# Sixteen more gathers in the front, three of them in flight across a change of pools, and top-16 operations of several lists taking turns

## The chip, the cores and the metric

The kernel runs on one core of one Trainium2 chip. The metric is the device time of one execution in microseconds; the median of three runs is given. The engines are named as in the profile: PE (matrix multiplication), DVE (vector), ACT (activation functions), POOL (here it only issues gathers) and SP (it issues the other transfers).

## The reference

One decoder layer over 512 tokens of width 1024: an attention of two groups of eight heads, a projection, a layer norm, then a lookup of experts (PEER), and a layer norm.

```python
def hybrid_mixer(x, w_in, w_out):
    proj = x @ w_in                       # q, k, v of both head groups
    oa = dilated_window_attention(qa, ka, va)     # heads "a": three dilated windows
    ob = stick_breaking_attention(qb, kb, vb)     # heads "b": cumulative log-sigmoids
    return concat(merge_heads(oa), merge_heads(ob)) @ w_out

def peer_ffn(x, w_query, sub_keys, expert_u, expert_v):
    q = (x @ w_query).reshape(b, s_len, 8, 2, 128)
    scores = einsum('bshpc,hpnc->bshpn', q, sub_keys)      # two lists of 128 per head
    top_s, top_i = top_k(scores, 16)
    cand_s = top_s[..., 0, :, None] + top_s[..., 1, None, :]   # 256 candidates per head
    best_s, best_pos = top_k(cand_s.reshape(..., 256), 16)
    expert_idx = take_along_axis(cand_i, best_pos)          # 128 experts per token
    gates = softmax(best_s)
    h = einsum('td,ted->te', x, expert_u[expert_idx])
    return einsum('te,ted->td', gates * gelu(h), expert_v[expert_idx])

x = layer_norm(ALPHA * x + hybrid_mixer(x, ...))
x = layer_norm(ALPHA * x + peer_ffn(x, ...))
```

## The kernel before, in words

The 512 tokens are four blocks of 128 (tb 0 to 3). For blocks 0 and 1 the experts' rows are gathered: one gather brings, for each of 128 tokens, the row of its j-th expert, 128 x 1024 numbers, 512 KB. That is 128 gathers of `peer_u` and 128 of `peer_v` for each block, 512 in all (`NG`). `gathers` keeps up to GB1 - 1 = 4 of them in flight with the first set of buffers, and some more once a second set (`g2`) is open; POOL issues them (L706). `gather_use` consumes them on DVE: a multiply with a running sum for a u row (L715), a multiply-add for a v row (L724, the first one L721). After the last u row of a block a Gelu on ACT turns the sums into gates (L717). Blocks 2 and 3 go through all experts instead ("dense"): chunks of 128 experts, with h matmuls (L821) and y matmuls (L1074), and gates from one-hot matrices (the gate stage). "h parts" of this dense work are put into earlier stages by `run_ahead`.

In time the program goes so:

- Block 0 goes first alone: projection, heads, output projection, layer norm, query, top-16, routing (`route_steps`), so that its gathers can begin at about 150 us.
- The front, 200 to 298 us: block 0's first `PRE0` gathers, the input projection of blocks 1 to 3 (weights split in two parts, L124) and the dilated heads of blocks 1 and 2 take turns in the proportion `MIXB`. Up to here a scheduler that inserts waits works on the written order. `limit` says up to which gather issues are allowed. At the end the old pools are closed and those of the next stages opened in their memory.
- The attention loop, 298 to about 500 us, under a manual schedule: 32 tasks, a head each, first the dilated heads of block 3 ("a") and the stick-breaking heads of block 1 ("b") alternating, then those of blocks 2 and 3. Each task takes one, two or three gathers. DVE's operations for a head are the masks with maximum (L318), the log parts (L349), and a division (L365); PE's are L315, L325, L331 (dilated) and L339 to L359 (stick-breaking). `load_out` loads the output weights before the loop. From task 20 the output projection (L492) and the normalization of block 1 are filled in, from task 28 those of block 2.
- The query loop, 500 to 634 us: 18 steps; step `it` multiplies the query of one list for blocks 1 to 3 (`q_mm`), the scores of the list before (`q_scores`, L593), and the top-16 of the list before that (`topk16`, L524 to L528, once for each of three blocks), with a gather after each of the three and `QH` h parts at its end.
- `route_steps(2)`, 634 to 672 us; then the gate stage, 672 to 806 us, with `route_steps` of blocks 3 and 1 in it; the main loop over the chunks of experts with the remaining gathers, 826 to 1483 us; the end.

Each engine runs its instructions in its own order, which is the order of the code in the manually scheduled part. In the names of tiles `su` is a head's scores, `nm` the negative maximum, `g` a gathered row set, `hg` the running sums of the u rows, `x` block 0's tokens, `yg` a second accumulator, `sc` the scores of a list.

Of the kernel before, what the change touches and what calls it, by code (L numbers as in the profile page):

```python
# [10 lines left out]
F32 = mybir.dt.float32  # L11
# [5 lines left out]
OP = mybir.AluOpType  # L17
# [3 lines left out]
P = 128  # L21
S = 512
D = 1024
# [3 lines left out]
NH = 8  # L27
# [39 lines left out]
PARTS = (0,), (1, 2, 3)  # L67
# [9 lines left out]
PRE0 = 52  # L77
QGATH = 3
QH = 3
# [4 lines left out]
GB1, GB2 = 5, 4  # L84
NG = 4 * P
GEND = P - 8
WBUF = 4
# [6 lines left out]
def build(ctx, nc, tc, a):  # L94
# [61 lines left out]
    def stats_steps(st):  # L156
        mv = keep.tile([P, 2], F32, name="mv", bufs=2)
        nc.vector.bn_aggr(mv, st.rearrange("p a b -> p (a b)"))
        w = keep.tile([P, 4], F32, name="lw", bufs=2)
        nc.vector.tensor_scalar_add(w[:, 0:1], mv[:, 1:2], EPS)  # L160
        nc.scalar.activation(w[:, 1:2], w[:, 0:1], AF.Ln)
        nc.scalar.activation(w[:, 2:3], w[:, 1:2], AF.Exp, scale=-0.5)
        yield
# [316 lines left out]
    def load_out():  # L480
        for c in range(2):
            for kq in range(4):
                wo[c, kq] = wop.tile([P, 2, 512], F32, name=f"wo{c}{kq}")
                nc.sync.dma_start(wo[c, kq], a["w_out"][c, kq])

# [10 lines left out]
    def normalize(tb):  # L496
        t = [] if tb == 0 else ln1
        if not t:
            for n in ("ln1_g", "ln1_b"):
                t.append(wst.tile([P, D], F32, name="w", bufs=WBUF) if tb == 0 else wop.tile([P, D], F32, name=n))  # L500
                nc.sync.dma_start(t[-1], a[n].to_broadcast([P, D]))
        r = x2[:, tb]
        s_ = stats_steps(sts[tb])
        next(s_)
# [3 lines left out]
        for g in range(2):  # L508
            sl = slice(g * 512, (g + 1) * 512)
            nc.vector.scalar_tensor_tensor(r[:, sl], r[:, sl], mv[:, 0:1], t[0][:, sl], op0=OP.subtract, op1=OP.mult)  # L510
            nc.vector.scalar_tensor_tensor(r[:, sl], r[:, sl], rs, t[1][:, sl], op0=OP.mult, op1=OP.add)
# [10 lines left out]
    def topk16(tb, i, sc):  # L522
        s2 = rq.tile([P, P], F32, name="s2", bufs=3)
        nc.vector.max(top[tb][:, i, 0:8], sc)  # L524
        nc.vector.max_index(topi[tb][:, i, 0:8], top[tb][:, i, 0:8], sc)  # L525
        nc.vector.match_replace(s2, top[tb][:, i, 0:8], sc, FMIN)
        nc.vector.max(top[tb][:, i, 8:16], s2)
        nc.vector.max_index(topi[tb][:, i, 8:16], top[tb][:, i, 8:16], s2)  # L528

# [67 lines left out]
    def route_steps(tb, h0=0, n=PH):  # L597
# [4 lines left out]
        def rt(shape, nm, dt=F32):  # L602
            return rq.tile(shape, dt, name=nm, bufs=1)
# [14 lines left out]
        for h in range(n):  # L618
            c2 = rq.tile([P, NCAND], F32, name="c2", bufs=2)
            nc.vector.max(best[:, h, 0:8], cand[:, h])  # L620
            nc.vector.max_index(posu[:, h, 0:8], best[:, h, 0:8], cand[:, h])
            nc.vector.match_replace(c2, best[:, h, 0:8], cand[:, h], FMIN)
            nc.vector.max(best[:, h, 8:16], c2)
            nc.vector.max_index(posu[:, h, 8:16], best[:, h, 8:16], c2)
            yield
        gt_ = (gate0, gate1)[tb][:, ks].rearrange("p (h k) -> p h k", h=n) if tb < 2 else rt([P, n, 16], "gate")
        nc.vector.tensor_sub(gt_, best, best[:, :, 0:1].to_broadcast([P, n, 16]))
        pos = rt([P, NK], "pos")
        nc.vector.tensor_copy(pos, posu.rearrange("p h k -> p (h k)"))
        posb = rt([P, NK], "posb", BF16)  # L630
        nc.vector.tensor_copy(posb, pos)
        t64 = rt([P, n, 16], "t64")
        nc.vector.tensor_scalar_mul(t64, topf[:, :, 0], 64.0)
        d0 = rt([P, n, 16], "d0")
        nc.vector.tensor_copy(d0[:, :, 0:1], t64[:, :, 0:1])
        nc.vector.tensor_sub(d0[:, :, 1:16], t64[:, :, 1:16], t64[:, :, 0:15])
# [22 lines left out]
        nc.vector.reduce_sum(gz, gt_, axis=AX.X)  # L659
        nc.vector.reciprocal(gz, gz)  # L660
        nc.vector.tensor_mul(gt_, gt_, gz[:, :, None].to_broadcast([P, n, 16]))
        nc.vector.tensor_sub(bo, bo, pos)
        nc.vector.tensor_scalar(i1, bo, 1.0 / 64.0, MAGIC, op0=OP.mult, op1=OP.add)
# [65 lines left out]
    limit = 0  # L729
# [135 lines left out]
    limit = PRE0  # L865
# [31 lines left out]
    with tc.manual_schedule():  # L897
        def take(n):
            for _ in head(gs, n):
# [3 lines left out]
                 [(k_, 3 if k_ == "a" else 1, h) for h in range(NH) for k_ in "ab"] + [("b", tb, h) for tb in (2, 3) for h in range(NH)]]  # L903
# [3 lines left out]
        load_out()  # L907
        for i in range(-1, NTASK + 2):
# [3 lines left out]

            new = i + 1 < NTASK
# [25 lines left out]
            if (fill_at := {20: 1, 28: 2}.get(i)):  # L939
                fill = chain(fill, project_out(fill_at), normalize(fill_at))  # L940
# [24 lines left out]
        for it in range(18):  # L965
# [7 lines left out]
            if it >= 2:  # L973
                for t, tb in enumerate(PARTS[1]):
                    topk16(tb, it - 2, scs[it - 2][:, t])
                    if t < QGATH:
                        take(1)
            else:
                take(2)
# [226 lines left out]
```

## Time and profile before

| what | value |
|---|---|
| median of 3 runs | 1584.94 us (1584.32 to 1587.28) |
| profiled execution, own time | 1586.14 us |
| its span | 1584.3 us |
| granted PE clock, mean | 0.935 |
| PE busy | 1433.4 us (90%) |
| DVE busy | 1223.2 us (77%) |
| ACT busy | 507.8 us (32%) |
| POOL busy | 686.0 us (43%) |
| HBM read | 477.78 MB, 312 GB/s over the span |

The profile is one execution. A busy share is an average over stages with different limits; a stage is read by its own window. The granted clock is the share of full speed that the throttle let PE have. A line of waits says which engine and line waited for which engine and line: total, times, longest, in us. A line of the timeline gives start, duration, engine, line and operation, and in brackets the idle time before it and what ended it.

### The profile page before, as it was taken

Reading aid. Unit: us, or ns where it says so; the run is one execution under the profiler, and the core shown is the slowest. Engines: PE = TensorE matmul, PEld = TensorE weight load, DVE = VectorE, ACT = ScalarE, POOL = GpSimd, SP = SyncE. Lnnn points to the kernel's source line nnn. Section 1 sums busy time; section 2 is a strip of 40 time slices with the busy share of each in tenths; the row PEclk is TensorE's granted clock in tenths of the full one; section 3 lists DMA queues with packets and bytes.
Section 4 is the critical chain, followed back from the end, with each engine's and each line's share of the span. In section 5 each row is a group of like instructions: output and inputs, shape, how many; then the busy total and the mean of one; then the engine's idle time right before and its main releaser. Section 6 shows DMA issues by size and latency. Waiting matters only on the chain.

```text
span 1584.3 us, 19704 instructions
## 1 busy us (share of the span) xinstructions
PE 1433.4 (90%) x6686; PEld 1143.9 (72%) x6686; DVE 1223.2 (77%) x2473; ACT 507.8 (32%) x1067; POOL 686.0 (43%) x526
## 2 busy tenths in 40 slices
PE   7988889799999999299969999999999999999896
PEld 3557777578658998178758887778777777777685
DVE  0138988346767999999978888778787878888987
ACT  1422333335421111199952222212222222222352
POOL 0001475335453333202537665566565656656500
PEclk9899999857999999699989999999999999999998
DMA  8657797466688888458979999999999999999972
GB/s 288 207 190 247 273 338 279 182 253 218 209 290 286 292 278 288 136 164 260 303 244 396 410 409 409 410 410 409 410 409 410 409 409 410 410 408 409 400 266 92
DMA packets 163220, 495.94 MB, mean 313 GB/s; under 512 B 15376, under 2 KB 48288, under 8 KB 163120
## 3 DMA queue, kind: packets, MB, share of 16 engines
q0 software_dynamic: 74304, 270.13, 45.9%
q1 hardware_dynamic: 87872, 223.90, 38.7%
q8 instruction: 53, 0.87, 0.2%
q10 hardware_dynamic: 944, 0.66, 0.1%
q14 instruction: 47, 0.39, 0.1%
HBM read 477.78 MB, written 16.84 MB: 312 GB/s over the span
## 4 chain that ended last, share of the span: by engine, by line
DMA 33%; PE 29%; DVE 25%; issue 7%; ACT 3%; POOL 2%; DVEq 0%; SPq 0%; ACTq 0%; POOLq 0%
DMA g<-peer_u,eidx 16%; DMA g<-peer_v,eidx 14%; PE y L1074 6%; PE h L821 4%; DVE x L724 3%; DVE yg L724 3%; POOL g L706 2%; DVE o L778 2%; PE m L262 2%; PE m L492 1%; DVE vl L124 1%; PE tr L492 1%; PE h L331 1%; PE h L359 1%; DVE topi L525 1%
## 5 line engine op out<-in xcount | busy, mean ns | idle before, releaser
L706 POOL DMA_INDIRECT g<-peer_u,eidx x256 | 336.3, 1314 | 427.1 <-DVE top L524 145.5
L706 POOL DMA_INDIRECT g<-peer_v,eidx x256 | 343.9, 1343 | 378.2 <-DVE yg L724 110.6
L821 PE MATMUL h<-xf,w 128*128 128x256 f32 x2048 | 478.8, 384 | 21.2 <-ACT gl L813 21.2
L821 PEld LDWEIGHTS h<-xf,w 128*128 128x128 f32 x2048 | 388.4, 193 | 76.6 <-ACT gl L813 22.5
L715 DVE SCALAR_TENSOR_TENSOR g<-g,x 128x1024 f32<-128x1024 f32 x256 | 308.3, 1222 | 86.8 <-DMA g<-peer_u,eidx 86.3
L1074 PE MATMUL y<-vh,a 128*128 128x512 f32 x928 | 294.0, 422 | 28.9 <-ACT a L1060 27.5
L1074 PEld LDWEIGHTS y<-vh,a 128*128 128x128 f32 x928 | 174.3, 193 | 83.5 <-ACT a L1060 39.3
L724 DVE SCALAR_TENSOR_TENSOR yg<-g,hg,yg 128x1024 f32<-128x1024 f32 x126 | 161.2, 1280 | 27.5 <-DMA g<-peer_v,eidx 26.9
L724 DVE SCALAR_TENSOR_TENSOR x<-g,hg,x 128x1024 f32<-128x1024 f32 x128 | 163.8, 1280 | 21.8 <-DMA g<-peer_v,eidx 21.4
L1060 ACT ACTIVATE a<-gl 128x512 fp32r<-128x512 f32 x58 | 36.5, 630 | 418.6 <-DVE gl L1054 418.6
L124 DVE TENSOR_TENSOR vl<-v,vh 128x1024 fp32r<-128x1024 f32 x122 | 148.9, 1221 | 19.7 <-ACT vh L1029 19.6
L1074 PE MATMUL y<-vl,a 128*128 128x512 f32 x464 | 149.5, 404 | 10.3 <-DVE vl L124 10.3
L1029 ACT ACTIVATE vh<-v 128x1024 fp32r<-128x1024 f32 x122 | 128.5, 1054 | 26.5 <-PE y L1074 14.4
L1074 PEld LDWEIGHTS y<-vl,a 128*128 128x128 f32 x464 | 86.2, 192 | 36.5 <-DVE vl L124 19.2
L787 ACT ACTIVATE o<-o1b,sg 128x128 f32<-128x128 bf16 x256 | 83.7, 401 | 5.8 <-DVE o1b L772 5.7
L813 ACT ACTIVATE gl<-h 128x256 f32<-128x256 f32 x128 | 47.7, 375 | 106.2 <-PE h L821 106.1
L262 PE MATMUL m<-w,x0f 128*128 128x256 f32 (+1 forms) x128 | 49.3, 529 | 8.7 <-DMA x0f<-xT 7.5
L793 PEld LDWEIGHTS m<-o,o 128*128 128x128 f32 x304 | 40.2, 201 | 17.3 <-ACT o L787 12.5
L793 PE MATMUL m<-o,o 128*128 128x128 f32 x304 | 44.0, 291 | 8.7 <-ACT o L787 4.4
L128 PE MATMUL m<-wl,x2h 128*128 128x512 f32 x96 | 41.8, 435 | 11.0 <-DVE wl L124 10.9
L778 DVE TENSOR_TENSOR o<-sg,c_small 128x512 f32<-128x512 f32 x64 | 44.1, 689 | 0.9 <-PE b L793 0.5
L262 PEld LDWEIGHTS m<-w,x0f 128*128 128x128 f32 x128 | 24.6, 204 | 26.4 <-issue 12.3
(259 smaller groups left out, 1926.4 us busy)
## 6 DMA issues: line engine op xcount, KB each, us to landing
w<-uT SPq DMA_DIRECT2D x128, 512.0 KB, 8.8
v<-peer_v SPq DMA_DIRECT2D x128, 512.0 KB, 7.2
w<-w_in SPq DMA_DIRECT2D x47, 512.0 KB, 5.7
gt<-gd SPq DMA_DIRECT2D x15, 960.0 KB, 11.7
w<-peer_wq SPq DMA_DIRECT2D x16, 512.0 KB, 4.3
wq<-peer_wq SPq DMA_DIRECT2D x16, 512.0 KB, 6.7
gd<-stage SPq DMA_DIRECT2D x15, 512.0 KB, 5.2
gd<-stage SPq DMA_DIRECT2D x15, 448.0 KB, 3.2
```

Of the source, the lines that this page charges most:

```text
L124: nc.vector.tensor_sub(parts[1], src, parts[0].bitcast(F32))
L262: nc.tensor.matmul(ps[:, ch * wd:(ch + 1) * wd], x0f[:, kk], w[:, k], start=kk == 0, stop=kk == KD - 1)
L706: nc.gpsimd.indirect_dma_start(out=u, out_offset=None, in_=a["peer_v" if kind else "peer_u"], in_offset=bass.IndirectOffsetOnAxis(ap=eidx[ ...
L715: nc.vector.scalar_tensor_tensor(u, u, 1.0, x, op0=OP.mult, op1=OP.mult, accum_out=hs[:, j:j + 1])
L724: nc.vector.scalar_tensor_tensor(acc, u, hs[:, j:j + 1], acc, op0=OP.mult, op1=OP.add)
L778: nc.vector.tensor_tensor(hot2[s], gate[tb][1][:, 0, t:t + TG, None].to_broadcast([P, TG, P]), iota[:, None, :].to_broadcast([P, TG, P]), ...
L787: nc.scalar.activation(hot[s][:, j], o1b[:, :, j], AF.Copy, scale=gate[tb][1][:, 1, t + j:t + j + 1])
L793: nc.tensor.matmul(gps[s][:, j * P:(j + 1) * P], o2[:, j], o1[:, j], start=True, stop=True)
L813: nc.scalar.activation(gls[c // 2][:, c % 2], ps[:, :ND], AF.Gelu)
L821: nc.tensor.matmul(hps[c][:, :ND], us[c][:, k], xf[:, k], start=k == 0, stop=k == KD - 1)
L1029: nc.scalar.activation(vsp[c][0], vs[c], AF.Copy)
L1074: nc.tensor.matmul(yps[t][hf], s_, w_[:, hf * 512:(hf + 1) * 512], start=c == 0 and n == 0, stop=c == P - 1 and n == len(terms) - 1)
```

## The change

- `PRE0` goes from 52 to 68, and `limit` in the front to 68 + GB1 - 1 = 72, so that gathers may be issued beyond the ones that the front consumes. By the order of instructions, 71 are issued before the second set of buffers opens, and 68 are consumed in the front; the other three are consumed in the attention loop.
- `load_out` becomes a generator that is moved on by one piece a task, and the layer norm's constants follow in it.
- The tasks of the attention loop stand in another order: two dilated heads first, then two stick-breaking heads for each dilated one, then two dilated ones, then as before. The output projection of block 1 is filled in from task 16.
- `normalize` does its first pass, (x - mean) times the gain, before it waits for the reciprocal of the deviation.
- In the query loop the five operations of the three blocks' top-16 take turns, and `QH` is 2.
- In `route_steps` the five operations of two heads' top-16 take turns, and some small operations stand in another order.

In the attention loop's beginning DVE had (L715 consumes a gather; `g_2274` and `g_2276` are the first two in the second set of buffers):

```order
353 L318 ISA su,nm<-a,c_maska 128x512
354 L318 ISA nm 128x1
355 L715 SCALAR_TENSOR_TENSOR g_2274,hg<-g_2274,x_97 128x1024
356 L715 SCALAR_TENSOR_TENSOR g_2276,hg<-g_2276,x_97 128x1024
357 L349 SCALAR_TENSOR_TENSOR su<-b,su 128x256
358 L318 ISA su,nm<-m_2308,c_maska 128x512
```

and has now (L739 is the same line in the changed file; `g_2314` is the first in the second set):

```order
358 L318 ISA su,nm<-a,c_maska 128x512
359 L318 ISA nm 128x1
360 L739 SCALAR_TENSOR_TENSOR g,hg<-g,x_97 128x1024
361 L318 ISA su,nm<-b,c_maska 128x512
362 L318 ISA nm 128x1
363 L739 SCALAR_TENSOR_TENSOR g,hg<-g,x_97 128x1024 x2
364 L349 SCALAR_TENSOR_TENSOR su<-m_2342,su 128x256
365 L739 SCALAR_TENSOR_TENSOR g_2314,hg<-g_2314,x_97 128x1024
366 L349 SCALAR_TENSOR_TENSOR su<-m_2361,su 128x256
```

The masks of two dilated heads and the log part of the first stick-breaking head now stand ahead of the first gather in the second set.

POOL's order at the same place was

```order
11 L753 DMA su<-c_maskb 128x128
12 L706 DMA g<-peer_u,eidx_99 128x1024 x52
13 L706 DMA g_2274<-peer_u,eidx_99 128x1024
14 L706 DMA g_2276<-peer_u,eidx_99 128x1024
15 L706 DMA g<-peer_u,eidx_99 128x1024 x5
```

and is now

```order
11 L777 DMA su<-c_maskb 128x128
12 L730 DMA g<-peer_u,eidx_99 128x1024 x64
13 L730 DMA g<-peer_u,eidx_100 128x1024 x7
14 L730 DMA g_2314<-peer_u,eidx_100 128x1024
15 L730 DMA g<-peer_u,eidx_100 128x1024 x5
```

71 gathers stand ahead of the first in the second set, where 52 stood.

In the query loop DVE had, for two of a step's three lists (L524 and L527 find maxima, L525 and L528 their places, L526 strikes them out):

```order
519 L524 MAX top_3153<-sc 128x8
520 L525 MAX_INDEX topi_3154<-top_3153,sc 128x8
521 L526 MATCH_REPLACE s_3427<-top_3153,sc 128x128
522 L527 MAX top_3153<-s_3427 128x8
523 L528 MAX_INDEX topi_3154<-top_3153,s_3427 128x8
524 L721 TENSOR_SCALAR yg<-g,hg 128x1024
525 L524 MAX top_3155<-sc 128x8
526 L525 MAX_INDEX topi_3156<-top_3155,sc 128x8
527 L526 MATCH_REPLACE s_3436<-top_3155,sc 128x128
```

and has now (L534, L536, L538, L540, L542 are the same five):

```order
514 L534 MAX top_3202<-sc 128x8
515 L534 MAX top_3204<-sc 128x8
516 L534 MAX top_3206<-sc 128x8
517 L748 SCALAR_TENSOR_TENSOR x_97<-g,hg,x_97 128x1024
518 L536 MAX_INDEX topi_3203<-top_3202,sc 128x8
519 L536 MAX_INDEX topi_3205<-top_3204,sc 128x8
520 L536 MAX_INDEX topi_3207<-top_3206,sc 128x8
521 L748 SCALAR_TENSOR_TENSOR yg<-g,hg,yg 128x1024
522 L538 MATCH_REPLACE s_3458<-top_3202,sc 128x128
523 L538 MATCH_REPLACE s_3460<-top_3204,sc 128x128
524 L538 MATCH_REPLACE s_3462<-top_3206,sc 128x128
```

No operation follows at once on the one whose result it needs; the gathers' multiplies moved between the rounds.

The diff, cut:

```diff
-PRE0 = 52
+PRE0 = 68
 QGATH = 3
-QH = 3
+QH = 2
...
                 wo[c, kq] = wop.tile([P, 2, 512], F32, name=f"wo{c}{kq}")
                 nc.sync.dma_start(wo[c, kq], a["w_out"][c, kq])
+                yield
+        for n in ("ln1_g", "ln1_b"):
+            ln1.append(wop.tile([P, D], F32, name=n))
+            nc.sync.dma_start(ln1[-1], a[n].to_broadcast([P, D]))
+            yield
...
-        next(s_)
+        mv = next(s_)
+        halves = [slice(g * 512, (g + 1) * 512) for g in range(2)]
+        for sl in halves:
+            nc.vector.scalar_tensor_tensor(r[:, sl], r[:, sl], mv[:, 0:1], t[0][:, sl], op0=OP.subtract, op1=OP.mult)
         if tb:
             yield
         mv, rs = next(s_)
-        for g in range(2):
-            sl = slice(g * 512, (g + 1) * 512)
-            nc.vector.scalar_tensor_tensor(r[:, sl], r[:, sl], mv[:, 0:1], t[0][:, sl], op0=OP.subtract, op1=OP.mult)
+        for sl in halves:
             nc.vector.scalar_tensor_tensor(r[:, sl], r[:, sl], rs, t[1][:, sl], op0=OP.mult, op1=OP.add)
...
+        for h in range(0, n, 2):
+            for i, _ in enumerate(mix(best_ops(h), best_ops(h + 1), (1, 1))):
+                if i in (4, 9):
+                    yield
...
-    limit = PRE0
+    limit = PRE0 + GB1 - 1
...
-                 [(k_, 3 if k_ == "a" else 1, h) for h in range(NH) for k_ in "ab"] + [("b", tb, h) for tb in (2, 3) for h in range(NH)]]
+                 [("a", 3, 0), ("a", 3, 1)] + [x_ for g_ in range(4) for x_ in (("b", 1, 2 * g_), ("b", 1, 2 * g_ + 1), ("a", 3, g_ + 2))]
+                 + [("a", 3, 6), ("a", 3, 7)] + [("b", tb, h) for tb in (2, 3) for h in range(NH)]]
...
-        load_out()
+        lo_ = load_out()
...
+            next(lo_, None)
...
-            if (fill_at := {20: 1, 28: 2}.get(i)):
+            if (fill_at := {16: 1, 28: 2}.get(i)):
...
-                for t, tb in enumerate(PARTS[1]):
-                    topk16(tb, it - 2, scs[it - 2][:, t])
-                    if t < QGATH:
+                ops = [topk_ops(tb, it - 2, scs[it - 2][:, t]) for t, tb in enumerate(PARTS[1])]
+                for r in range(5):
+                    for o_ in ops:
+                        next(o_)
+                    if r < QGATH:
                         take(1)
```

`topk_ops` and `best_ops` hold the same five operations as before, with a `yield` after each.

More of the change, by code (lines that the diff above doesn't have):

```diff
@@ L162, in stats_steps @@
         nc.scalar.activation(w[:, 2:3], w[:, 1:2], AF.Exp, scale=-0.5)
-        yield
+        yield mv
         nc.vector.tensor_mul(w[:, 3:4], w[:, 2:3], w[:, 2:3])
@@ L497, in normalize @@
         t = [] if tb == 0 else ln1
-        if not t:
+        if tb == 0:
             for n in ("ln1_g", "ln1_b"):
-                t.append(wst.tile([P, D], F32, name="w", bufs=WBUF) if tb == 0 else wop.tile([P, D], F32, name=n))
+                t.append(wst.tile([P, D], F32, name="w", bufs=WBUF))
                 nc.sync.dma_start(t[-1], a[n].to_broadcast([P, D]))
@@ L522, in topk16, with topk_ops @@
     def topk16(tb, i, sc):
+        for _ in topk_ops(tb, i, sc):
+            pass
+    def topk_ops(tb, i, sc):
         s2 = rq.tile([P, P], F32, name="s2", bufs=3)
         nc.vector.max(top[tb][:, i, 0:8], sc)
+        yield
         nc.vector.max_index(topi[tb][:, i, 0:8], top[tb][:, i, 0:8], sc)
+        yield
         nc.vector.match_replace(s2, top[tb][:, i, 0:8], sc, FMIN)
+        yield
         nc.vector.max(top[tb][:, i, 8:16], s2)
+        yield
         nc.vector.max_index(topi[tb][:, i, 8:16], top[tb][:, i, 8:16], s2)
+        yield
     def keys(c):
@@ L617, in route_steps, with best_ops @@
         posu = rt([P, n, 16], "posu", U32)
-        for h in range(n):
+        def best_ops(h):
             c2 = rq.tile([P, NCAND], F32, name="c2", bufs=2)
             nc.vector.max(best[:, h, 0:8], cand[:, h])
+            yield
             nc.vector.max_index(posu[:, h, 0:8], best[:, h, 0:8], cand[:, h])
+            yield
             nc.vector.match_replace(c2, best[:, h, 0:8], cand[:, h], FMIN)
+            yield
             nc.vector.max(best[:, h, 8:16], c2)
+            yield
             nc.vector.max_index(posu[:, h, 8:16], best[:, h, 8:16], c2)
             yield
+        for h in range(0, n, 2):
+            for i, _ in enumerate(mix(best_ops(h), best_ops(h + 1), (1, 1))):
+                if i in (4, 9):
+                    yield
         gt_ = (gate0, gate1)[tb][:, ks].rearrange("p (h k) -> p h k", h=n) if tb < 2 else rt([P, n, 16], "gate")
-        nc.vector.tensor_sub(gt_, best, best[:, :, 0:1].to_broadcast([P, n, 16]))
         pos = rt([P, NK], "pos")
         nc.vector.tensor_copy(pos, posu.rearrange("p h k -> p (h k)"))
+        t64 = rt([P, n, 16], "t64")
+        nc.vector.tensor_scalar_mul(t64, topf[:, :, 0], 64.0)
         posb = rt([P, NK], "posb", BF16)
         nc.vector.tensor_copy(posb, pos)
-        t64 = rt([P, n, 16], "t64")
-        nc.vector.tensor_scalar_mul(t64, topf[:, :, 0], 64.0)
         d0 = rt([P, n, 16], "d0")
+        nc.vector.tensor_sub(d0[:, :, 1:16], t64[:, :, 1:16], t64[:, :, 0:15])
         nc.vector.tensor_copy(d0[:, :, 0:1], t64[:, :, 0:1])
-        nc.vector.tensor_sub(d0[:, :, 1:16], t64[:, :, 1:16], t64[:, :, 0:15])
+        nc.vector.tensor_sub(gt_, best, best[:, :, 0:1].to_broadcast([P, n, 16]))
         nc.vector.tensor_add(d0, d0, small[:, None, 16:32].to_broadcast([P, n, 16]))
@@ L659, in route_steps @@
         nc.vector.reduce_sum(gz, gt_, axis=AX.X)
+        nc.vector.tensor_sub(bo, bo, pos)
         nc.vector.reciprocal(gz, gz)
+        nc.vector.tensor_scalar(i1, bo, 1.0 / 64.0, MAGIC, op0=OP.mult, op1=OP.add)
         nc.vector.tensor_mul(gt_, gt_, gz[:, :, None].to_broadcast([P, n, 16]))
-        nc.vector.tensor_sub(bo, bo, pos)
-        nc.vector.tensor_scalar(i1, bo, 1.0 / 64.0, MAGIC, op0=OP.mult, op1=OP.add)
         nc.vector.tensor_scalar(i1, i1, MAGIC, None, op0=OP.subtract)
```

## The prediction

> **What bounds the kernel now.** I cut the span into stages first, since the limit changes from stage to stage. The columns are: the stretch, its length, busy time of PE, PEld, DVE, ACT and POOL, the granted PE clock, the DMA engines' share, GB/s.
>
> ```profile
> span 1584.3 us, 19704 instructions
> ...
> 200.00:268.00 68.00, 58.42 (x275) 47.07 (x274) 55.77 (x108) 23.29 (x47) 47.92 (x35) 0.90 0.94 333
> 268.00:298.00 30.00, 28.55 (x173) 23.42 (x174) 13.08 (x29) 12.60 (x31) 0.52 (x1) 1.00 0.10 35
> 298.00:310.00 12.00, 4.77 (x22) 2.47 (x21) 3.15 (x7) 3.50 (x8) 9.04 (x10) 0.74 0.95 367
> 310.00:372.00 62.00, 61.59 (x214) 47.56 (x214) 30.29 (x63) 24.24 (x56) 23.57 (x19) 0.50 0.66 240
> 500.00:634.00 134.00, 130.96 (x749) 118.56 (x747) 128.46 (x439) 21.17 (x44) 44.86 (x48) 0.99 0.87 295
> 634.00:672.00 38.00, 6.66 (x16) 4.41 (x16) 36.46 (x116) 3.83 (x10) 9.86 (x9) 0.60 0.42 136
> 672.00:806.00 134.00, 121.50 (x744) 102.66 (x745) 129.76 (x352) 121.70 (x350) 38.12 (x20) 0.97 0.76 238
> 889.00:1483.00 594.00, 564.65 (x2454) 461.02 (x2453) 485.17 (x617) 138.47 (x221) 359.54 (x268) 0.99 1.03 409
> ```
>
> The main loop (889 to 1483) is bound by DMA: share 1.03 at 409 GB/s, and 29.35 us of PE idle. One 512 KB transfer, a gather or a load, costs 524288 / 409000 = 1.28 us there. The front (200 to 298) has two halves: DMA full until 268, then DMA at 0.10 while PE is at 28.55 of 30 and DVE at 13.08. The query loop (500 to 634) and the routing behind it (634 to 672) are DVE's.
>
> Next I read the waits around 300, then DVE's and PE's timeline there.
>
> ```profile
> POOL g L706 <- ACT qB L299: 29.7, 1, 29.7
> DVE g L715 <- DMA g<-peer_u,eidx: 8.3, 3, 6.5
> PE b L351 <- DVE su L349: 7.6, 1, 7.6
> ...
> 306.23 1.23 DVE L715 SCALAR_TENSOR_TENSOR g<-g,x 128x1024 f32<-128x1024 f32 x1 [6.55 <-DMA g<-peer_u,eidx]
> 308.79 1.23 DVE L715 SCALAR_TENSOR_TENSOR g<-g,x 128x1024 f32<-128x1024 f32 x1 [1.33 <-DMA g<-peer_u,eidx]
> ...
> 313.59 2.07 PE L315 MATMUL a<-kA,qA 64*128 64x512 f32 x2
> 321.75 2.07 PE L315 MATMUL m<-kA,qA 64*128 64x512 f32 x2
> ```
>
> POOL cannot start the first gather of the second set of buffers until the old pool's memory is free (29.7 us), so that gather is issued at 298 and lands at 306; DVE stands in front of it, L349 behind it in DVE's order, and PE stands 7.6 us for L349. From there the granted clock is 0.50: a pair of head tasks takes 321.75 - 313.59 = 8.16 us with PE busy throughout. The clock follows windows of 3.41 us:
>
> ```profile
> 64.89:68.30 3.41, 2.83 (x14) 1.87 (x14) 1.46 (x3) 2.52 (x12) 0.00 (x0) 1.00 0.67 250
> 68.30:71.71 3.41, 3.41 (x14) 2.46 (x13) 0.58 (x2) 1.58 (x6) 0.00 (x0) 0.50 0.00 0
> ...
> 300.40:303.81 3.41, 2.37 (x11) 1.18 (x11) 0.00 (x0) 2.14 (x6) 2.51 (x3) 1.00 0.97 359
> 303.84:307.25 3.41, 0.00 (x0) 0.00 (x0) 1.02 (x1) 0.00 (x0) 2.50 (x4) 0.50 1.02 404
> 375.54:378.96 3.42, 3.42 (x26) 2.92 (x25) 1.63 (x4) 1.83 (x5) 2.81 (x3) 1.00 0.78 225
> ```
>
> Earlier, in block 0's heads, it dropped after a window with 2.83 of 3.41 us busy; here after one with 2.37, though the idle time in that was one us, and it stayed low for 62 us in which PE was busy for 61.59 (the fourth row of the stages), until 375.5, in b2's heads with their wider matmuls.
>
> **The change, part by part.** Own time is 1586.14 us, 1.84 around the span of 1584.3; the median of the runs is 1584.94, so I subtract 1.2 at the end.
>
> *Gathers in the front (52 to 68, and three in flight).* By the order of POOL's instructions each later point is 16 gathers further on, and 19 at the main loop's first chunk (201 done before, 220 now; the last three because fewer h parts, QH 2, let the remainder loop take more). So the main loop keeps 292 of 311. 19 x 1.28 = 24.3 us less DMA in a stretch with 29.35 us of PE idle. PE's floor is a chunk of 3.45 + 2.77 = 6.22 us,
>
> ```profile
> 826.49 3.45 PE h L821 x16
> 829.94 2.77 PE y L1074 x12
> ```
>
> against 594 us for 463 transfers (594 us at 409 GB/s), that is 87 chunks of two loads and some 3.3 gathers at 6.8 us. With 5 us between the saving and PE's floor, and a tenth lost to waits for ACT and DVE, I take -20 (ends 0 and -24.3).
>
> In the front the 16 gathers need 16 x 1.28 = 20.5 us of DMA and 16 x 1.23 (the multiply at 306.23) = 19.7 us of DVE. 268 to 298 has 27 us of DMA and 16.9 us of DVE to spare, so about 3 us stick out. The far end: they go at the pace of the first half, 68 us for 35 gathers (1.94 each, 31 us), all after the front's end. What a gather costs DVE in waiting there is 12.3 / 12, about 1 us:
>
> ```profile
> DVE g L715 <- DMA g<-peer_u,eidx: 12.3, 12, 2.0
> ...
> g<-peer_u,eidx POOLq DMA_INDIRECT x35, 6.4
> ```
>
> The waits fell to gathers in the full half; in the empty half they should vanish, so I take +2 (ends 0 and +31).
>
> *The start of the attention loop.* Now three landed gathers and both first heads' masks stand ahead of the first gather that POOL must wait for. The wait for it does not go away, since its issue still hangs on L299; it comes one head later, and PE has more work ahead of it. The output weights' loads stand at the same places of SP's queue and wait for the same memory, so I give the splitting 0. I take 3 us off the 7.65 (ends 0 and -7.6). The order of the tasks brings b1 to its end earlier and project_out(1), with matmuls 512 wide, at task 16 instead of 20. The clock came back at 375; it should at about 367, and 8 us at half rate are 4. Together -7. The far ends: the clock never drops, and PE needs 31 us for the 62 at 0.50, but the 19 gathers of that stretch (POOL's count) and the 8 weight pieces ahead of them want 27 x 1.28 = 35 us of DMA, so 62 - 35 = 27 us more; and 0, if the clock comes back where it does now.
>
> The Trainium skill ("TensorE: Matmul & The Clock Gate", Part 1, the two states) says that the clock falls after one idle window of about 3.4 us and returns after one busy one. The trace agrees on the window's length, not on the rest: it fell after a window 69% busy and stayed at 0.50 through 62 / 3.41 = 18 windows in which PE was nearly always busy. By that rule the 62 us here would have cost a few, and a stall under 3.4 us nothing; the second half of that is a rival below.
>
> *Table loads.* The Gelu of block 0's sums falls between the normalizations, and ACT's order has five more table loads, 1.283 us each:
>
> ```profile
> L657 ACT ACT_TABLE_LOAD x3 | 3.8, 1283 | 0.1
> ```
>
> That is 6.4 us of ACT. The two normalizing passes that go ahead of Ln and Exp hide some; I take +1 (ends 0 and +6.4).
>
> *Query loop.* Three lists take turns, so that no operation of a list follows the one it needs. Starts in the trace of before:
>
> ```profile
> 547.12 0.29 DVE L524 MAX8 top<-sc 128x8 f32<-128x128 f32 x1
> 547.45 0.09 DVE L525 MATCH_VALUE_LOAD topi<-top,sc 128x8 f32 x1
> 547.52 0.29 DVE L525 FIND_INDEX8 topi<-top,sc 128x8 uint32<-128x128 f32 x1
> 547.73 0.07 DVE L526 MATCH_VALUE_LOAD s<-top,sc 128x8 f32 x1
> 547.78 0.28 DVE L526 MATCH_REPLACE8 s<-top,sc 128x128 f32<-128x128 f32 x1
> 548.10 0.29 DVE L527 MAX8 top<-s 128x8 f32<-128x128 f32 x1
> 548.42 0.09 DVE L528 MATCH_VALUE_LOAD topi<-top,s 128x8 f32 x1
> ...
> 555.42 0.28 DVE L524 MAX8 top<-sc 128x8 f32<-128x128 f32 x1
> ```
>
> Where the next needs the result the step is 0.32 to 0.33 us (547.12 to 547.45, 547.78 to 548.10, 548.10 to 548.42); where it doesn't (the index at 547.52, then the value load at 547.73) it is 0.21, 0.08 before the first ends. Three such steps a list, 0.11 to 0.12 each, are 0.35; 16 x 3 lists give 16.8 us. A loop step takes 555.42 - 547.12 = 8.30 us on DVE and would take 7.25. PE is ahead of DVE: its last score matmul is at 601.1, DVE's last list ends at 631.7.
>
> ```profile
> L593 PE MATMUL m<-skT,qT x96: 272/275/275, 497.7 to 601.1; 128*128 128x128 f32 x96
> ...
> 631.42 0.28 DVE L528 FIND_INDEX8 topi<-top,s 128x8 uint32<-128x128 f32 x1
> ```
>
> So DVE's saving is the stage's. DMA's 295 GB/s would become 338, under 409, though its share of 0.87 comes near 1; for that I take -15 (ends 0 and -16.8). One h part less a step lightens PE, which is not the bound; the four left over come before the main loop, 4 x 2 matmuls of 0.22 us, +1 with their wait.
>
> *Routing in pairs.* One head takes 639.46 - 638.29 = 1.17 us:
>
> ```profile
> 638.29 0.19 DVE L620 MAX8 best<-cand 128x8 f32<-128x50 f32 x1
> 638.52 0.09 DVE L621 MATCH_VALUE_LOAD posu<-best,cand 128x8 f32 x1
> 638.72 0.07 DVE L622 MATCH_VALUE_LOAD c<-best,cand 128x8 f32 x1
> ...
> 639.46 0.19 DVE L620 MAX8 best<-cand 128x8 f32<-128x50 f32 x1
> ```
>
> 0.23 us where the next needs it, 0.12 where not; three steps, 0.34 us a head, 2.7 for 8 heads, some more from the small operations in another order. Block 0's routing -2.5 (DVE is full there), block 2's -3 (PE idles). The gate stage holds blocks 3 and 1, 5.5 to 7 us of DVE, but ACT is at 121.70 and PE at 121.50 of 134, so I take half, -3 (ends 0 and -7).
>
> The Trainium skill ("VectorE: DVE Perf Modes", The DRAIN you can't avoid) says that after every DVE operation the next does not start until the pipeline is empty, and its table advises against arranging chained operations for speed. Taken strictly, taking turns would give nothing and the sum would be 23.5 us smaller. The steps of 0.21 against 0.33 in the rows above speak against it, though each pair there is also of other operations.
>
> **Sum.** +2 - 2.5 - 7 + 1 - 15 + 1 - 3 - 3 - 20 = -46.5. 1586.1 - 46.5 - 1.2 = 1538.4 us.
>
> **The rivals.**
>
> *The clock holds.* If the first windows of the attention loop stay fuller than the 69% of 300.40, the stage runs at the full clock: 27 us more, 1511. For it: the stall is shorter and comes later. Against: DMA is full there (0.95 from 298 to 310), gathers land 2.56 us apart (306.23, 308.79), and a task takes one; PE's 2.04 us for it at the full clock (8.16 / 4) fill 80% of that, less than the 83% of the window at 64.89 after which it fell. A shorter cold stretch lies between, 1525. This is also what the skill's rule on the clock would give for a short stall.
>
> *Taking turns gives nothing.* The short steps belong to those pairs of operations, not to their independence: 15 + 2.5 + 3 + 3 = 23.5 us back, 1562.
>
> *The front grows.* DVE runs in written order, and the 16 gathers go at 1.94 us behind the front's end: 31 in place of 2, 1567.
>
> *The main loop doesn't take it.* PE's floor or the chunk's own waits eat the freed DMA: 20 back, 1558.
>
> *Slower.* In the front each added multiply stands ahead of a head's mask, and if each waits for a whole landing (6.4 us by the row above, less the 1.23 of the multiply that goes on, 5.2) the 16 cost 83 us: 1538 + 81 = 1619. It turns slower from 46.5 / 16 + 0.1 = 3.0 us a gather. Against it stands the wait of about 1 us in the fuller half.
>
> **How the numbers follow.** Two times of this kernel differ measurably from about 0.2% on, 3.2 us. Forecast 1538 (with the terms' ends, 1528 to 1548): 0.53. Clock held or nearly so, 1505 to 1527: 0.20. No gain from turns, 1562: 0.08. Longer front, 1567: 0.08. Main loop without gain, 1558: 0.07. Slower: 0.03; no change, several losses at once: 0.01. The range 1507 to 1559 leaves out the three highest cases and half a tenth at the low end, under 0.2 in all. Faster 0.96, same 0.01, slower 0.03.
>
> **What the profile after would show.** The gap of PE before L351 shorter than 7.65 us, and a stretch at clock 0.50 that ends within some 60 us; the query step at 7.25 us on DVE; the main loop still at DMA share about 1.03 but some 20 us shorter; five more table loads; DMA well above 0.10 in the front's second half. I am wrong if a step of the query loop is still 8.3 us, if the front ends much later against its start, or if the chunks stay at 6.8 us.

## The result, and the profile after

The changed kernel takes 1545.2 us (median of four runs, 1541.1 to 1545.7); the ratio to the kernel before is 0.9745, 95% interval 0.9722 to 0.9768. The profiled execution took 1545.74 us, its span 1544.0. 40.3 us of span are gone where 46.5 were forecast, and the sum hides one step, the attention loop, that went the other way. The windows below are of the changed kernel, cut at its own stages; the columns are the stretch, its length, busy time of PE, PEld, DVE, ACT and POOL, the granted PE clock, the DMA share, and GB/s.

```profile
200.00:268.00 68.00, 58.59 (x266) 47.75 (x265) 54.94 (x106) 22.84 (x47) 45.31 (x35) 0.87 0.93 330
268.00:301.00 33.00, 31.51 (x187) 25.44 (x187) 28.49 (x57) 13.66 (x33) 27.21 (x18) 1.00 0.84 270
301.00:313.00 12.00, 4.57 (x22) 3.00 (x22) 7.00 (x15) 2.35 (x6) 7.07 (x7) 0.66 0.97 360
313.00:380.00 67.00, 65.87 (x220) 49.17 (x221) 32.52 (x64) 27.79 (x65) 26.93 (x24) 0.50 0.69 251
511.00:626.00 115.00, 115.00 (x690) 105.59 (x689) 113.54 (x433) 19.60 (x41) 46.13 (x50) 1.00 0.92 324
626.00:661.00 35.00, 14.81 (x57) 11.36 (x55) 34.45 (x120) 4.93 (x10) 9.07 (x8) 0.69 0.59 201
661.00:792.00 131.00, 123.48 (x773) 108.54 (x774) 126.23 (x354) 122.81 (x356) 38.87 (x20) 0.97 0.78 250
869.00:1443.00 574.00, 558.92 (x2474) 464.95 (x2473) 466.00 (x604) 141.82 (x224) 341.71 (x254) 0.99 1.03 409
```

The query loop is shorter and DVE still full in it; the main loop is shorter at the same 409 GB/s. The front's second half now has DMA at 0.84 instead of 0.10. The start of the attention loop is as poor as it was: 4.57 of 12 us on PE, and then the clock at 0.50, up to 380 instead of 375.

For a comparison by stage I took, in each trace, the starts of the same instructions: the first 512-wide mask matmul of a block 3 head (the attention loop's first, 297.8 before and 300.9 after), the last score matmul of a head (442.5 and 451.0), the first list's score matmul (497.7 and 511.1), the last index of the lists (631.4 and 625.7), the first and last one-hot operation of the gate stage, the last h matmul (1470.8 and 1433.4, in the main loop), and the end. The differences of after and before, beside the forecast:

```
                          before    after   change   forecast
up to the attention loop   297.8    300.9    +3.1     -0.5  (+2 - 2.5)
attention loop             199.9    210.2   +10.3     -6    (-7 + 1)
query loop                 133.7    114.6   -19.1    -14    (-15 + 1)
routing of block 2          39.7     35.1    -4.6     -3
gate stage                 135.6    130.8    -4.8     -3
main loop and the end      777.6    752.4   -25.2    -20
span                      1584.3   1544.0   -40.3    -46.5
```

### The profile page after: what moved, and what is told of

The parts are those of the page before. It is cut to its first block, busy times and chain, and to the rows that moved or that the text cites. A ratio compares the mean times of both kernels' runs of the same rounds, so it can differ in the third digit from the quotient of the medians.

```text
span 1544.0 us, 19751 instructions
## 1 busy us (share of the span) xinstructions
PE 1422.9 (92%) x6686; PEld 1146.1 (74%) x6686; DVE 1199.3 (78%) x2473; ACT 513.9 (33%) x1072; POOL 686.4 (44%) x526
## 4 chain that ended last, share of the span: by engine, by line
DMA 36%; PE 27%; DVE 19%; issue 8%; ACT 5%; POOL 3%; SPq 0%; ACTq 0%; POOLq 0%; DVEq 0%
DMA g<-peer_u,eidx 18%; DMA g<-peer_v,eidx 15%; PE y L1102 6%; PE h L845 5%; POOL g L730 3%; DVE yg L748 3%; DVE x L748 2%; ACT o L811 2%; PE m L262 2%; DVE vl L124 1%; PE m L497 1%; PE h L331 1%; PE h L566 1%; DVE s L538 1%; PE tr L497 1%
## 5 line engine op out<-in xcount | busy, mean ns | idle before, releaser
L730 POOL DMA_INDIRECT g<-peer_u,eidx x256 | 339.8, 1327 | 402.6 <-DVE topi L542 146.4
L739 DVE SCALAR_TENSOR_TENSOR g<-g,x 128x1024 f32<-128x1024 f32 x256 | 308.3, 1222 | 86.6 <-DMA g<-peer_u,eidx 86.4
L837 ACT ACTIVATE gl<-h 128x256 f32<-128x256 f32 x128 | 48.0, 376 | 153.8 <-PE h L845 153.7
L817 PEld LDWEIGHTS m<-o,o 128*128 128x128 f32 x304 | 39.5, 195 | 12.3 <-ACT o L811 10.3
```

Source lines behind the costliest of these rows:

```text
L730: nc.gpsimd.indirect_dma_start(out=u, out_offset=None, in_=a["peer_v" if kind else "peer_u"], in_offset=bass.IndirectOffsetOnAxis(ap=eidx[ ...
L739: nc.vector.scalar_tensor_tensor(u, u, 1.0, x, op0=OP.mult, op1=OP.mult, accum_out=hs[:, j:j + 1])
L817: nc.tensor.matmul(gps[s][:, j * P:(j + 1) * P], o2[:, j], o1[:, j], start=True, stop=True)
L837: nc.scalar.activation(gls[c // 2][:, c % 2], ps[:, :ND], AF.Gelu)
```

## The experiments

The kernels below ran in three groups of four, each group on one chip beside runs of the kernel before; ratios are to those. "Loop" is the attention loop as in the table, "low" the time between 290 and 510 us in which the granted clock was below 0.75, counted in windows of 1 us: 77 us before, 95 after. There is one profile of each kernel, and a stage moves from one to the next: eight profiles with 68 gathers and without idle matmuls, two of them of the changed kernel itself, have loops of 204.6 us (low 82) to 213.7 us (low 102). About half of the difference in low time shows in the loop, as half rate would give. So I go by the ratio first and by the stage second, and a difference of a few us in the loop says nothing unless it lies outside that spread.

**52 gathers in the front again, all else as changed.**

```diff
-PRE0 = 68
+PRE0 = 52
-    limit = PRE0 + GB1 - 1
+    limit = PRE0
```

> The changed kernel with 52 gathers in the front and none in flight beyond them (as before), all else as changed. Theory A (the added gathers fill the time in which DMA was idle at the end of the front, but the transfers that then crowd the start of the attention loop come later; net a main loop 16 gathers shorter, paid for in part by a longer attention loop): main loop about 16 x 1.28 = 20 us longer, front 3 us shorter, attention loop some 5 to 10 us shorter, total about 1553 to 1558. Rival B (the longer attention loop is the new order of the tasks, and the added gathers cost nothing there): attention loop as long as in the changed kernel, total 1562 to 1566. Rival C (the Gelu of block 0 among the normalizations is what costs; it goes back into the query loop here): as A in the total, but all of the difference after 440 us and none between 300 and 440.

Ratio 0.9811 (0.9785 to 0.9837), 1556.3 us. The main loop is 21 us longer than in the changed kernel (663.0 against 641.8), 1.3 us for each of 16 gathers; so far theory A has its size. The loop is 202.2 us (low 81 us), 8 less than in the profile above but 2.4 under the nearest profile with 68 gathers. By parts: up to the last score matmul of a head it took 145.6 us, inside the 144.5 to 153.7 with 68 gathers; from there to the last output matmul 42.8, below their 45.5 to 46.8. These 3.4 us only change place: the query loop is 117.6 us, 3.0 more, since block 0's Gelu is in it again (at 504.1) with a wait of DVE of 2.7 us. So a loss ahead of the heads' end, as theory A had it, is not shown; where the difference is clear it lies behind the heads, as rival C had it.

**None in flight beyond the front.**

```diff
-    limit = PRE0 + GB1 - 1
+    limit = PRE0
```

> The changed kernel with 68 gathers in the front, but none issued beyond them before the second set of buffers opens. Theory A: the three in flight had not landed when DVE came to them (waits of 3.2 us and 1.4 us), so they move the wait, they do not remove it: total within 3 us of 1545. If they help as the prediction assumed (first heads are not held up): 3 to 8 us slower, 1548 to 1553. If they harm, because the first masks stand behind them in DVE's order: 3 to 8 us faster.

Ratio 0.968 (0.9647 to 0.9713); the changed kernel run again on another chip gave 0.9704 (0.9655 to 0.9753). Loop 208.7 us. No difference that these runs can tell from zero: what the three in flight save is not seen. The trace says why. The gather that DVE waits 3.2 us for in the changed kernel is not one of the three but the 68th, the front's last; the first of the three is the next one, with the wait of 1.4. The 68th is there without the three as well: DVE waits 3.14 us for it, and PE 7.9.

**The tasks in the old order.**

```diff
-                 [("a", 3, 0), ("a", 3, 1)] + [x_ for g_ in range(4) for x_ in (("b", 1, 2 * g_), ("b", 1, 2 * g_ + 1), ("a", 3, g_ + 2))]
...
+                 [(k_, 3 if k_ == "a" else 1, h) for h in range(NH) for k_ in "ab"] + [("b", tb, h) for tb in (2, 3) for h in range(NH)]]
...
-            if (fill_at := {16: 1, 28: 2}.get(i)):
+            if (fill_at := {20: 1, 28: 2}.get(i)):
```

> The changed kernel with the tasks of the attention loop in the order of before (a and b alternating) and block 1's output projection filled in from task 20 again. Theory A: the order matters little, total 1542 to 1548, the clock back at about 380 us as now. Rival B (the order costs the 10 us that the attention loop grew by): total about 1535 to 1538. If the earlier fill brings the clock back earlier, as the prediction had it: 1549 or more.

Ratio 0.9714 (0.9686 to 0.9742), loop 207.4 us, low 89 us. The order costs nothing that can be told, and it gains nothing: the clock came back at 371.5 us, 80 us after the loop's start. In the changed kernel's two profiles that was 79 and 74 us, and 71 to 79 in the other kernels in which it fell there.

**No change of table among the normalizations.**

```diff
-                nc.scalar.activation(hs, hs, AF.Gelu)
+                nc.scalar.activation(hs, hs, AF.Exp if tb == 0 else AF.Gelu)
```

> The changed kernel with Exp in place of the Gelu on block 0's sums, so that block 0's gates hold other numbers and ACT has no table to change among the normalizations. Rival C (the five added table loads and the waits on them cost): 4 to 7 us faster, 1538 to 1541, all of it between 465 and 511 us. Theory A: 0 to 2 us faster, since DVE and PE wait there for the output projection and for landings.

Ratio 0.9689 (0.966 to 0.9719), loop 206.6 us. From the heads' end (the last score matmul) to the last output matmul it took 45.5 us, 46.2 in the changed kernel, 40.9 before. So the table loads are some 0.7 of the 5.3 us that this part grew by. What the rest is shows in the waits of the changed kernel there (engine and line, what it waited for, total, times, longest), and in ACT's and PE's timeline:

```profile
DVE hg L742 <- ACT hg L741: 7.5, 1, 7.5
```

```profile
468.40 0.60 ACT L355 ACTIVATE su<-m 128x512 f32<-128x512 f32 x1 [5.89 <-PE m L353]
469.01 1.28 ACT L741 ACT_TABLE_LOAD   x1
470.31 0.31 ACT L741 ACTIVATE hg<-hg 128x128 f32<-128x128 f32 x1
...
477.57 1.11 PE L173 MATMUL tr<-c_ident,o 128*128 128x128 f32 x4 [5.76 <-ACT o L370]
```

The Gelu stands in ACT's order behind the last head's L355, which waits for PE. DVE, whose last u row was done at 463.1, waits 7.5 us for it with the second half of block 2's output and its statistics behind; ACT's next steps wait for those, and PE for ACT. With Exp in its place DVE waited 6.1 us at the same point: it is the place in the order, not the table.

**Matmuls whose result nobody reads, to hold the clock.**

```diff
+        warm = bank("m2")
+
+        def dummy(n):
+            for _ in range(n):
+                nc.tensor.matmul(warm, tri, maska, start=True, stop=True)
...
             next(lo_, None)
+            if 0 <= i < 12:
+                dummy(14 if i == 0 else 2 if i < 5 else 1)
```

> The changed kernel with idle matmuls (512 wide, into an unused bank, results unused): 14 where PE waits at the start of the attention loop, then 2 a task for four tasks and 1 a task up to task 11. Theory A (the attention loop is long because the clock is at half after that wait: it was so for some 95 us between 290 and 510, against 77 before): if they hold the clock, the loop shrinks from 210 us to 180 to 190 and the total to 1515 to 1527. If the clock falls all the same, the 29 idle matmuls cost about 0.55 to 1.1 us each, less the 7 us of waiting they fill: 10 to 20 us slower. Rival D (DMA, not the clock, sets the pace there): the clock holds and the loop stays at 205 to 212.

Ratio 0.9643 (0.9589 to 0.9696), 1529.1 us; the changed kernel beside it 1539.1. The clock held from 301 to 390 (low 21 us in all), the loop fell to 195.4. The loop stays 5 us above the forecast and the total 2, but the sign and the place are as theory A says: its windows are

```profile
301.00:313.00 12.00, 12.00 (x32) 5.25 (x30) 4.62 (x10) 1.41 (x3) 6.15 (x6) 1.00 0.96 366
313.00:380.00 67.00, 66.31 (x330) 42.25 (x330) 41.13 (x80) 32.55 (x74) 31.58 (x27) 1.00 0.80 282
```

With the same gathers and heads to do, DMA is no fuller than 0.96 and 0.80, and DVE does 41.13 us of work in the 67 where it did 32.52. So the clock set the pace there, not DMA (rival D). It fell later on for 6.8 us (at 394.9) and for 13.7 (at 456.4).

**The output weights one piece a task, in fact.** SP runs ahead of the tasks: in the changed kernel it issued all eight weight pieces in 4.82 us.

```profile
300.54 4.82 SPq L484 DMA_DIRECT2D wo<-w_out  x8
```

```diff
-                nc.sync.dma_start(wo[c, kq], a["w_out"][c, kq])
+                nc.scalar.dma_start(wo[c, kq], a["w_out"][c, kq])
...
-            nc.sync.dma_start(ln1[-1], a[n].to_broadcast([P, D]))
+            nc.scalar.dma_start(ln1[-1], a[n].to_broadcast([P, D]))
```

> The changed kernel with the output weights and the norm's constants issued by ACT, one piece in each task in ACT's order, in place of all by SP at once at 300.5. Theory A with the crowd of transfers as its cause: the gathers in flight land earlier, DVE's waits of 3.2 and 1.4 us and PE's of 7.2 us at the start shrink by half or more, attention loop 204 or less, total 1536 to 1541; if the clock then holds, 1520. Rival (the gathers alone fill DMA there, or the tiles' memory is what they wait for): no change within 3 us.

Ratio 0.968 (0.9631 to 0.9728), the changed kernel beside it 0.9704: not told apart. Loop 205.9 us, low 86, inside the spread. DVE's first wait for a landing is 3.24 us as before, PE's wait 7.4; the later waits are gone. So theory A's cause was half right: the weights do delay the gathers that follow, but not the 68th. It was issued at 294.72, with one piece of the weights beside it, and took 7.9 us to land where the three before it took 5.2 to 5.4; with all eight pieces beside it, in the changed kernel, it took 7.7 after 5.0 to 5.9. What makes it slow was not settled.

```profile
302.63 1.23 DVE L739 SCALAR_TENSOR_TENSOR g<-g,x 128x1024 f32<-128x1024 f32 x1 [3.24 <-DMA g<-peer_u,eidx]
```

**The three lists one after the other.**

```diff
-                for r in range(5):
-                    for o_ in ops:
-                        next(o_)
+                for r, o_ in enumerate(ops):
+                    for _ in o_:
+                        pass
                     if r < QGATH:
                         take(1)
```

> The changed kernel with the three lists' top-16 one after the other again. By the steps of the trace (0.33 us after the operation that is needed, 0.21 otherwise) the query loop, 114.6 us, becomes 131 to 132, total 17 us more, 1561 to 1563. If the shorter steps belong to the pairs of operations and not to independence: no change. If the 4 us beyond the 16.8 that the loop gained come from the fewer h parts: 131, not 134.

1559.8 us against 1539.1 beside it; ratio 0.9835 (0.9783 to 0.9888). The query loop took 132.6 us, 18.0 more than with turns (114.6 to 114.8 in eight of the other kernels' profiles); the rest of the 20.7 lies outside it, 4 us of it in the attention loop. The remaining 1.1 us to the 133.7 of before is what the rest of the change does in this loop, the smaller QH and the Gelu's move out of it among it.

**The changed kernel once more.**

> The changed kernel itself once more, beside the other three on one chip. 0.9745 of before, within 0.3%; the attention loop between 206 and 211 us, since in the runs so far it moved by some us with the place of the clock's windows.

1539.1 us, ratio 0.9704 (0.9655 to 0.9753); loop 204.6 us, under the span that I had given, low 82 us.

**One head after the other in the routing.**

```diff
-        for h in range(0, n, 2):
-            for i, _ in enumerate(mix(best_ops(h), best_ops(h + 1), (1, 1))):
-                if i in (4, 9):
-                    yield
+        for h in range(n):
+            for _ in best_ops(h):
+                pass
+            yield
```

> The changed kernel with one head's top-16 after the other in all routing. By the steps (0.23 us after the operation that is needed, 0.12 otherwise): 2.7 us in block 0's routing before the first gather, 3 to 4 of the routing of block 2 (35 us now, 39 then), 3 to 5 of the gate stage (131 now, 135 then): 8 to 11 us slower in all. If ACT and PE set the gate stage's pace, as the prediction had it in part: 131 to 133 there, 6 to 8 in all.

1547.3 us, ratio 0.9738 (0.9709 to 0.9767), not told apart from the changed kernel's 0.9745 and 0.9704; the loop, which has nothing to do with it, is the longest of all at 213.7 (low 102). So only the stages answer: block 2's routing 37.8 us (35.1 with pairs), the gate stage 134.8 (130.8, and 130.0 to 131.2 in the others), 2.7 and 4.0 us. The steps would give 16 x 0.34 = 5.4 us for the 16 heads in the gate stage. It pays most of that, so DVE sets its pace for the larger part, for all that ACT and PE are nearly full there. In block 0's routing nothing is seen: from its start to the first gather it takes 18.6 us (130.5 to 149.1), as with pairs.

**Fewer idle matmuls, with and without the paced weights.**

```diff
-            if 0 <= i < 12:
-                dummy(14 if i == 0 else 2 if i < 5 else 1)
+            if 0 <= i < 7:
+                dummy(14 if i == 0 else 1)
```

> As the kernel with idle matmuls, with fewer of them: 14 at the wait and 1 a task up to task 6, in place of 29 in all 20. If the clock still holds: 9 matmuls of about 0.5 us less, the attention loop at 190 to 192 us, total some 5 us under the first. If it falls again before task 16: loop 200 or more.

1521.7 us, ratio 0.9579 (0.954 to 0.9617); loop 187.1, low 21 us. The last nine had only cost time: the loop is 8.3 us shorter without them. An idle matmul stands as two matmuls in the trace (58 for the 29), and 15 of these took 6.60 us on PE, 0.44 each; so the nine took 9 x 0.88 = 7.9 us. The second has 12 at the wait in place of 14, and the weights issued by ACT as above:

> The two together: 12 idle matmuls at the wait, 1 a task up to task 6, and the output weights issued by ACT a piece a task. If the gathers land earlier and the clock holds, the attention loop is 186 to 190 us and the total 1516 to 1524; if what holds it is the number of idle matmuls, it falls and the loop is over 200; if the pacing adds nothing under a full clock, the same as with fewer idle matmuls alone.

1515.1 us, ratio 0.9543 (0.9513 to 0.9574), the fastest of all; loop 182.2 us, low 10 us. The loop is 4.9 us shorter than with fewer idle matmuls alone. That is not shown to be the pacing's: the time at half clock is also some 10 us less, which at half rate is 5 us, there are two idle matmuls fewer, and the intervals of the two ratios overlap. The windows answer to the two of the changed kernel above:

```profile
301.00:313.00 12.00, 12.00 (x35) 5.24 (x33) 5.58 (x11) 2.70 (x7) 4.86 (x6) 1.00 1.01 388
313.00:380.00 67.00, 66.31 (x353) 45.68 (x352) 44.87 (x88) 35.01 (x79) 35.61 (x30) 1.00 0.83 300
```

**52 gathers with the idle matmuls of the first such kernel.** The two edits are shown above.

> 52 gathers in the front, with the idle matmuls of the first such kernel. Theory A (the attention loop of the changed kernel is longer than with 52 because the clock is low for longer): with the clock held in both, the loop is within 2 us of the 195.4 it had with 68. Rival (the added gathers' backlog of transfers costs the loop directly): 5 or more us shorter than with 68, 190 or less. In both the main loop is 20 us longer than with 68.

1547.4 us, ratio 0.9735 (0.9707 to 0.9763); loop 192.0, against 195.4 with 68, between the two forecasts. By parts it is clear: up to the heads' end 134.6 against 134.8 us, the same; from there to the last output matmul 43.5 against 46.8. With the clock held the gathers cost the heads nothing; the 3.3 us are in the later part, where DVE waits 7.4 us for the Gelu with 68 gathers; with 52 the Gelu is in the query loop, which is 117.6 us against 114.7. The main loop is 663.1 us against 642.1, 21 us longer once more.

## Why the prediction was right or wrong

*Right: the time lies in the range and the sign is right.* The likeliest case, with the clock falling as before and coming back after some 60 to 80 us, is the one that came. That the time is so near is in part luck. The first two rows of the table came out 3.6 and 16.3 us worse than their terms, the other four 13.7 us better, and 6.2 is what is left.

*Main loop, -20, was -22.3 (-25.2 with the end).* The arithmetic of 19 transfers at 1.28 us held, nearly without the tenth I took off. With 52 gathers, 16 fewer, the main loop is 21.2 us longer, 1.3 a gather, at the same 1.03 of DMA, and 21.0 longer in the pair of kernels with idle matmuls.

*Query loop, -15 + 1, was -19.1; the turns alone 18.0.* Mis-sized low. DVE's steps after the change:

```profile
542.61 0.08 DVE L536 MATCH_VALUE_LOAD topi<-top,sc 128x8 f32 x1
542.68 0.28 DVE L536 FIND_INDEX8 topi<-top,sc 128x8 uint32<-128x128 f32 x1
542.88 0.07 DVE L536 MATCH_VALUE_LOAD topi<-top,sc 128x8 f32 x1
...
546.56 0.67 DVE L540 MAX8 top<-s 128x8 f32<-128x128 f32 x3
547.15 0.07 DVE L542 MATCH_VALUE_LOAD topi<-top,s 128x8 f32 x1
...
547.93 0.66 DVE L534 MAX8 top<-sc 128x8 f32<-128x128 f32 x3
```

A maximum costs 0.59 / 3 = 0.20 us in a row of three (546.56 to 547.15), where it cost 0.33 with its user behind it. The third of the row also has a value load behind it, but of another list, and its step is 0.19 (546.96 to 547.15): the same pair of operations is short when the second does not need the first. So it is independence and not the kind of pair that makes the step short. A step of the loop takes 547.93 - 540.84 = 7.09 us (the start of the same operation a step before, in the next fence), under the 7.25 forecast, and DMA at 0.92 had room, so the 1.8 us I kept back for it were not needed.

```profile
540.84 0.66 DVE L534 MAX8 top<-sc 128x8 f32<-128x128 f32 x3
```

The Trainium skill ("VectorE: DVE Perf Modes", The DRAIN you can't avoid) has the next operation wait for an empty pipeline after each one, and adds that a next operation that is not held starts earlier. The prediction took up the first half alone. This trace shows an earlier start: the value load of the next list's index search, at 542.88, starts while the search ahead of it (542.68 for 0.28) still runs. Taking turns is worth 18.0 us in the one loop, so the rival in which it gives nothing falls.

*Routing, -3 and -3, were -4.6 and -4.8.* Pairs account for 2.7 and 4.0. I had halved the gate stage's share because ACT and PE were nearly full there, and the run with one head after the other shows that DVE sets its pace for the larger part. The rest, about 1.9 and 0.8 us, I put down to the small operations' order, which was not tried alone. Block 0's -2.5 is not seen: its routing's start to the first gather took 18.9 us before (131.3 to 150.2) and 18.6 after (132.4 to 151.0), and the run with one head after the other has 18.6 too.

*Front, +2, was +3.1 in the profile* (with block 0's routing in it; the first multiply came at 158.7 and 158.8), which is not told from zero. From the first multiply to the attention loop it took 139.1 us before and 142.1 after, but 136.9 to 141.7 in the ten other profiles with 68 gathers, and 139.3 and 141.4 in the two with 52. The longer-front rival falls: the 18 gathers from 268 to 301 fit beside PE's 31.51 of 33 us, and DVE's waits for landings there came to 3.4 us in all.

```profile
DVE g L739 <- DMA g<-peer_u,eidx: 3.4, 6, 1.1
```

The price of a gather's wait that would have turned the sign, 3.0 us, is far from the 3.4 / 18 = 0.2 us measured.

*Attention loop, -7 + 1, was +10.3, and +4.7 in the second profile of the same kernel.* This is the step that failed: neither the shorter wait nor the earlier clock came. Up to the heads' end the two profiles took 150.2 and 144.5 us, 144.7 before; from there to the last output matmul 46.2 both times, 40.9 before.

First, "three landed gathers" was wrong. They were issued, not landed, and ahead of them and of the first head's mask stands the 68th gather, the front's own last, to which the prediction gave no wait. In the kernel before DMA had stood idle ahead of the changeover, and DVE was done with its 52 gathers at 274.6; with 16 gathers more the 68th is issued at 299.84 and was still under way at 304.2 when DVE came to it. These are POOL's and DVE's timelines and PE's wait:

```profile
299.84 0.94 POOL L730 DMA_INDIRECT g<-peer_u,eidx  x1 [0.31 <-issue]
...
307.54 1.23 DVE L739 SCALAR_TENSOR_TENSOR g<-g,x 128x1024 f32<-128x1024 f32 x1 [3.23 <-DMA g<-peer_u,eidx]
...
308.69 0.69 DVE L318 CUSTOM_DVE_ANT_0 su<-a,c_maska 128x512 f32<-128x512 f32 x1
```

```profile
PE a L325 <- ACT su L321: 7.2, 1, 7.2
```

7.2 us instead of 7.6: one wait took the other's place. Where I priced the wait that would be late next, I looked at the gather that waits for the pool and not at the ones ahead of it.

Second, the clock came back no earlier. These are the first stretch at half clock in the loop before, and the three after:

```profile
303.84:375.54 71.70, 65.13 (x225) 50.09 (x225) 35.73 (x70) 26.14 (x60) 30.54 (x26) 0.50 0.69 254
...
304.82:379.93 75.11, 68.29 (x228) 50.87 (x229) 36.21 (x72) 28.97 (x67) 30.88 (x28) 0.50 0.73 265
410.66:420.90 10.24, 9.55 (x33) 7.24 (x32) 5.28 (x10) 3.63 (x6) 4.90 (x4) 0.50 0.61 190
475.51:485.75 10.24, 6.80 (x17) 3.94 (x18) 6.63 (x11) 5.05 (x8) 3.66 (x4) 0.50 0.85 285
```

The fill at task 16 did bring project_out(1) to 376.4 from 386.4, but the first stretch is no shorter: 75.1 us against 71.7, and 68.3 in the second profile of the changed kernel. Before, and in that second profile (clock up at 372.3, first output matmul at 373.6), it ended ahead of any output matmul. So project_out is not needed for it, and the 4 us were for nothing. Most of the 18 us that the half clock lasted longer come from the two later falls, 20.5 us together where before they were 3.4 us each. At half rate 18 us are about 9 us of work; the second profile has 5 us more of low time than before, and up to the heads' end it is no longer than before. In the runs with the idle matmuls this part of the difference is gone. Whether the added gathers make the clock fall more often is not shown: low was 77 and 81 us with 52, 82 to 102 with 68.

Third, the Gelu. I counted the table loads (+1, end 6.4), and those measured 0.7; what I missed is that it stands in ACT's order behind a head's operation that waits for PE. With 52 gathers, the part behind the heads is 3.3 us shorter, and the query loop, to which the Gelu goes back, 3.0 longer; over both loops its place costs next to nothing. Of the 5.3 us that this part grew by, some 2 are there with 52 gathers too; what they are was not settled.

*The rival in which the clock holds, 1511.* It did not come, but its size was right: the idle matmuls hold the clock and with paced weights give 1515.1 us, some 24 us under the changed kernel's 1539.1, on another chip, by ratios 0.9543 against 0.9704; 27 had been worked out. It named a rule of the Trainium skill for a short stall ("TensorE: Matmul & The Clock Gate", Part 1); the stall was 7.2 us, so what a short one does was not seen. The other half of that rule, that one busy window of 3.4 us brings the clock back, does not describe this trace: from 313 to 380 PE was 65.87 of 67 us busy at 0.50.

## What to carry to other kernels

A transfer that is issued is not one that has landed: filling an idle stretch of DMA puts its last transfers in front of the next stage's first operations, so look at what will still be under way at that stage's start. Where several equal chains of short vector operations exist, let them take turns; a step costs by whether the next needs its result. And a wait of 7 us on PE can cost some 20 us more when the clock falls with it (loop 204.6 us against 187.1 and 182.2): here 18 or 20 matmuls that nobody reads paid for themselves, 12 or 14 of them at the wait, and nine more behind those only cost their own time.

## What the runs showed of the hardware

PE at half clock stayed there for 65 to 75 us although it was busy nearly throughout (65.87 of 67 us in the changed kernel), in every kernel without idle matmuls; with PE full of 512-wide idle matmuls over the 7 us wait (12.00 of 12 us busy) it did not fall there, and 18 of them, 12 at the wait, were enough. So the busy share alone does not tell whether the clock will rise; what in the heads' matmuls keeps it low was not tried.

On DVE the cost of an operation depends on whether the next one reads its result: 0.20 us for a maximum followed by another list's, 0.33 followed by its own user. And a transfer queued by SP ignores the order of the tasks: a loop that issues one piece per task issued all of them in 4.82 us, until an engine that follows the tasks issued them.
